# Feed-forward weights in seven-product units: sums by adding transfers in place of GpSimd subtractions

## The chip, the cores and the metric

The kernel runs on one core of a Trainium2 chip. The metric is the device time of one execution in microseconds. TensorE (PE) does the matrix products, ScalarE (ACT) and VectorE (DVE) work along rows, GpSimd (POOL) is a third elementwise engine, and SyncE (SP) issues most transfers.

## The reference

The kernel computes two decoder layers over a sequence of 512 tokens of width 1024 in fp32. Layer 0 mixes with a causal convolution, layer 1 with differential attention. Behind each follow a SwiGLU feed-forward block of inner width 2816 and a gated embedding. The change concerns the feed-forward block alone:

```python
def swiglu(x, w_gate, w_up, w_down):
    return (jax.nn.silu(x @ w_gate) * (x @ w_up)) @ w_down

h = h + swiglu(rms_norm(h, ffn_norm_g[i]), ffn_w_gate[i], ffn_w_up[i], ffn_w_down[i])
```

## The kernel before

All activations are held transposed, as eight chunks of 128 features by 512 tokens. Every fp32 operand is split into a high part, rounded to the matrix format by ScalarE (a cast), and a low part, the remainder, which VectorE subtracts. A product is then three matmuls (low by high, high by high, high by low; lines 166 to 168).

The inner width of 2816 is 22 chunks, taken in three parts of 6, 8 and 8 (`PARTS`). The first part is computed plainly. The second and third go in *units*. A unit computes two chunks of one matrix (a `Gate` unit or an `Up` unit) as a 2 x 2 block product: the weights are blocks A11, A12, A21, A22 of 512 by 128, the normalized activations are blocks B11, B12, B21, B22 of 512 by 256. Seven block products in place of eight give the four result blocks. They need four sums of weight blocks (S1 to S4) and four sums of activation blocks (T1 to T4). The T sums are made once per layer in `Operands.chunk`, the S sums once per unit. A part of 8 chunks is 8 units, Gate and Up in turn, so each layer has 16 units and the kernel 32.

For a unit, `load` (lines 699 to 706) fetches two raw tiles of 512 KB each through SyncE's queue: r0 holds A11 and A12, r1 holds A21 and A22. Gate units use the tiles A0 and A1, Up units two slots of `wraw`. `prep` then makes the operands in six steps:

- step 0 splits A11 and A12 (a 1024-wide cast, line 710, and a 1024-wide subtraction, line 711);
- step 1 makes S1 = A21 + A22 and S2 = S1 - A11 on GpSimd (lines 720 and 721);
- step 2 splits S1 and S2;
- step 3 makes S3 = A11 - A21 into a tile of its own (line 732) and S4 = A12 - S2 into A21's place (line 733), on GpSimd;
- step 4 splits S3 alone (512 wide, lines 736 and 737);
- step 5 splits S4 and A22 together.

The pairs of 1024 go to four buffers each (`whi`, `wlo`); S3's pair goes to the tiles A4 and A5 in turn. `p(i)` does product i, 12 pairs of weight load and matmul, and what follows from its result: copies out of PSUM by ScalarE (lines 760, 765, 767), additions by VectorE (lines 762, 768, 773), and `ready`, which applies Silu (line 783) or multiplies Gate by Up (line 794). Within a unit the products go in the order 1, 2, 6, 5, 7; products 4 and 3, which use A22 and S4, are put off into the next unit, behind its products 2 and 6. So a unit's stretch is 1, 2, 4 of the last, 6, 3 of the last, 5, 7. While one unit's products run, `run` traces the next unit's `prep` between them.

The order of instructions on each engine is made when the kernel is built, from the order of the code and estimated times of readiness; an engine then works its queue in order. The first unit of each part is prepared during the down projection of the part before it, at the places that `HOOKS` lists (output chunk: steps).

Of the kernel before, what the change touches and what calls it, by code (L numbers as in the profile page):

```python
# [14 lines left out]
AF = mybir.ActivationFunctionType  # L15
ALU = mybir.AluOpType
# [4 lines left out]
P = 128  # L21
S = 512
# [56 lines left out]
LA = 4  # L79
PACK = True  # L80
OPS_AT = (1, 2, 4, 5)
HOOKS = {5: (None,), 6: (1, 3), 7: (0, 2, 4, 5)}
HT = S // 2
E1 = True
GLO = 1
# [6 lines left out]
def trunk(ctx, tc, xT, pT, wts, diag, dww, vec, rel, onehot, lamv, out):  # L92
    nc = tc.nc
    V, A, G, T = nc.vector, nc.scalar, nc.gpsimd, nc.tensor
# [7 lines left out]
    def sb(shape, tag, bufs, dt=F32):  # L102
        uid[0] += 1
        return pool.tile(shape, dt, tag=tag, name=f"{tag}_{uid[0]}", bufs=bufs)
# [10 lines left out]
    f = lambda ap: ap.bitcast(F32)  # L115
# [6 lines left out]
    def col(name, i=0):  # L122
        a, _ = VEC[name]
        return vt[:, a + i : a + i + 1]
# [9 lines left out]
    t = wk()[:, 0:P]  # L134
# [4 lines left out]
    t = tp()  # L139
# [49 lines left out]
    def both(t):  # L189
        return t[:, 0], t[:, 1]  # L190
# [18 lines left out]
    class Norm:  # L209
# [11 lines left out]
        def chunk(self, c):  # L221
            self.split(c)
            if c == 0:
                self.acc = sb([P, S], "acc", 1)
                A.activation(self.acc, h[c], AF.Square)
            else:
                sq = wk()
                self.square = A.activation(sq, h[c], AF.Square)  # L228
                self.last = self.eng.tensor_tensor(self.acc, self.acc, sq, ALU.add)  # L229
# [57 lines left out]
    def load(c):  # L287
        return lambda: nc.sync.dma_start(h[c], xT[c])
# [308 lines left out]
    with tc.manual_schedule(engines={V.engine, A.engine}):  # L597
        for c in range(NC + 2):
            if c < NC:
# [3 lines left out]
                hi = A.copy(z[c][0], y[c])  # L603
            if c >= 2:
                lo = V.tensor_tensor(z[c - 2][1], y[c - 2], f(z[c - 2][0]), ALU.subtract)
# [46 lines left out]
    class Operands:  # L652
# [10 lines left out]
        def chunk(self, k, rb):  # L663
            ub = sb([P, 2, S], "B6", 1)
            u1, u2 = both(ub)
            for c, u in ((k, u1), (k + 4, u2)):
                V.scalar_tensor_tensor(u, h[c], col(self.norm.g, c), rb, ALU.mult, ALU.mult)
            (u11, u12), (u21, u22) = ((u[:, :HT], u[:, HT:]) for u in (u1, u2))
            hi1, lo1 = self.low[k]
            A.copy(hi1, u11)  # L670
            hi2, lo2 = self.uppers(k)
            A.copy(hi2, u2)
            t = sb([P, 4, HT], "B7", 1)
            V.tensor_tensor(t[:, 0], u12, u11, ALU.subtract)
            V.tensor_tensor(t[:, 1], u22, t[:, 0], ALU.subtract)
            V.tensor_tensor(t[:, 2], u22, u12, ALU.subtract)
            V.tensor_tensor(t[:, 3], u21, t[:, 1], ALU.subtract)
            hi, lo = self.tops(k)
            A.copy(hi, t)
            V.tensor_tensor(lo1, u11, f(hi1), ALU.subtract)  # L680
            self.at["B11"][k] = hi1, lo1
            V.tensor_tensor(lo2, u2, f(hi2), ALU.subtract)
            self.at["B21"][k] = hi2[:, :HT], lo2[:, :HT]
            self.at["B22"][k] = hi2[:, HT:], lo2[:, HT:]
            V.tensor_tensor(lo, t, f(hi), ALU.subtract)
            for i in range(4):
                self.at[f"T{i + 1}"][k] = hi[:, i], lo[:, i]

    class Unit:
# [9 lines left out]
        def load(self):  # L699
            self.raw = []  # L700
            for j in range(2):
                raw = sb([P, 2, S], *(("wraw", 2) if self.raws == "wraw" else (f"A{j}", 1)))
                nc.sync.dma_start(raw, wts[self.i + j].rearrange("p (j k) -> p j k", j=2))
                self.raw.append(raw)
            self.sums = sb([P, 2, S], f"A{2 + self.n % 2}", 1)
            self.s3 = sb([P, 2, S], f"A{6 + self.n % 2}", 1)[:, 0]

        def two(self, src, a, b):
            hi, lo = sb([P, 2, S], "whi", 4, F32R), sb([P, 2, S], "wlo", 4, F32R)
# [3 lines left out]
                self.w[n] = hi[:, j], lo[:, j]  # L713

        def prep(self, step):
            (r0, r1), s, s3 = self.raw, self.sums, self.s3
            if step == 0:
                self.two(r0, "A11", "A12")
            elif step == 1:
                G.tensor_tensor(s[:, 0], r1[:, 0], r1[:, 1], ALU.add)  # L720
                G.tensor_tensor(s[:, 1], s[:, 0], r0[:, 0], ALU.subtract)
            elif step == 2:
                if self.first:
                    for j in range(2):
                        hi, lo = wk(F32R), wk(F32R)
                        A.copy(hi, s[:, j])
                        V.tensor_tensor(lo, s[:, j], f(hi), ALU.subtract)
                        self.w[f"S{j + 1}"] = hi, lo
                else:
                    self.two(s, "S1", "S2")  # L730
            elif step == 3:
                G.tensor_tensor(s3, r0[:, 0], r1[:, 0], ALU.subtract)
                G.tensor_tensor(r1[:, 0], r0[:, 1], s[:, 1], ALU.subtract)
            elif step == 4:
                hi, lo = both(sb([P, 2, S], f"A{4 + self.n % 2}", 1, F32R))
                A.copy(hi, s3)
                V.tensor_tensor(lo, s3, f(hi), ALU.subtract)
                self.w["S3"] = hi, lo
            else:
                self.two(r1, "S4", "A22")  # L740

        def product(self, acc, w, b, first):
            for k in range(4):
# [4 lines left out]
        def p(self, i):  # L748
            if i == 1:
                self.a, self.c = mm(), mm()  # L750
            a, lo, hi = self.a[:, :HT], self.c[:, :HT], self.c[:, HT:]
            acc, w, b, first = {
                1: (a, "A11", "B11", True), 2: (hi, "A12", "B21", True), 6: (a, "S2", "T2", False),
                5: (lo, "S1", "T1", True), 7: (a, "S3", "T3", False), 4: (a, "A22", "T4", False),
                3: (lo, "S4", "B22", False),
            }[i]
            self.product(acc, w, b, first)
            o = self.out
            if i == 1:
                A.copy(o[0][:, :HT], a)  # L760
            elif i == 2:
                V.tensor_tensor(o[0][:, :HT], o[0][:, :HT], hi, ALU.add)
                self.ready(0, 0)
            elif i == 6:
                A.copy(o[0][:, HT:], a)
            elif i == 7:
                A.copy(o[1][:, HT:], a)
                V.tensor_tensor(o[1][:, HT:], o[1][:, HT:], lo, ALU.add)
                self.ready(1, 1)
            elif i == 4:  # L770
                self.ready(1, 0)
            elif i == 3:
                V.tensor_tensor(o[0][:, HT:], o[0][:, HT:], lo, ALU.add)
                self.ready(0, 1)

    class Gate(Unit):
# [3 lines left out]
        def ready(self, j, k):  # L780
            cut = slice(k * HT, (k + 1) * HT)
            src = self.a[:, :HT] if (j, k) == (1, 0) else self.out[j][:, cut]
            A.activation(self.out[j][:, cut], src, AF.Silu)

    class Up(Unit):
        def start(self):
# [3 lines left out]
        def ready(self, j, k):  # L790
            o, g = self.out[j], self.gate.out[j]
            cut = slice(k * HT, (k + 1) * HT)
            if j == 1:
                V.tensor_tensor(o[:, cut], self.a[:, :HT] if k == 0 else o[:, cut], g[:, cut], ALU.mult)
            self.done[j] += 1
            if self.done[j] < 2:
                return
            if j == 0:
                V.tensor_tensor(o, o, g, ALU.mult)
            hid = both(sb([P, 2, S], f"B{self.at + j}", 1, F32R))  # L800
            A.copy(hid[0], o)
            V.tensor_tensor(hid[1], o, f(hid[0]), ALU.subtract)
            self.hid[self.at + j] = hid

    def ffn(norm, after, spare):
# [14 lines left out]
        def run(us):  # L820
            for n, x in enumerate(us):
                last = us[n - 1] if n else None
                nxt = us[n + 1] if n + 1 < len(us) else None
                x.start()
                if nxt:
                    nxt.load()
                x.p(1)
                if nxt:
                    nxt.prep(0)
                x.p(2)  # L830
                if nxt:
                    nxt.prep(1)
                if last:
                    last.p(4)
                x.p(6)
                if nxt:
                    nxt.prep(2)
                if last:
                    last.p(3)
                x.p(5)  # L840
                if nxt:
                    nxt.prep(3)
                    nxt.prep(4)
                x.p(7)
                if nxt:
                    nxt.prep(5)
            us[-1].p(4)
            us[-1].p(3)

        us = None  # L850
        for at, (f0, n) in enumerate(PARTS):
# [34 lines left out]
            if at < len(PARTS) - 1:  # L886
# [6 lines left out]
                x = us[0]  # L893
                for m, steps in HOOKS.items():
                    hooks[m] = partial(lambda steps: [x.load() if k is None else x.prep(k) for k in steps], steps)
# [56 lines left out]
    for k in range(2):  # L952
        t = tp()
# [447 lines left out]
```

## Time and profile before

| | |
|---|---|
| median of 3 runs | 1249.71 us (1249.7 to 1250.26) |
| the profiled execution | 1249.66 us |
| its span | 1247.6 us |
| TensorE busy | 1236.4 us, 99% |
| VectorE busy | 877.6 us, 70% |
| ScalarE busy | 623.0 us, 50% |
| GpSimd busy | 470.5 us, 38% |
| granted TensorE clock | 0.999 |

The span is the part of the execution that the trace covers; the rest lies before and after it. A group of the profile is one line of the kernel, one engine, one operation and the tiles it writes and reads ("out<-in"), with the count, the busy time, the mean duration in ns, and the idle time of the engine just before.

### The profile page before, as it was taken

The numbers are of one execution on the slowest core, as the hardware profiler recorded it, in microseconds if no ns is written. First come the engines' busy times: TensorE is split into PE (matmuls) and PEld (weight loads), VectorE is DVE, ScalarE is ACT, GpSimd is POOL, SyncE is SP. The second block draws the span as 40 slices with busy tenths as digits, with TensorE's granted clock in tenths as the row PEclk, the third lists the DMA queues.
The fourth block names the chain that finished last, engine by engine and source line by source line (L and its number), as shares of the span: only waits on it lengthen the run. The fifth ranks groups of instructions, "written<-read, shape, count | busy, mean of one in ns | idle before, by whom it ended". The sixth has DMA issues, their size and how long they took to land.

```text
span 1247.6 us, 18420 instructions
## 1 busy us (share of the span) xinstructions
PE 1236.4 (99%) x7080; PEld 1081.5 (87%) x7080; DVE 877.6 (70%) x1230; ACT 623.0 (50%) x1096; POOL 470.5 (38%) x355
## 2 busy tenths in 40 slices
PE   9999999999999999999999999999999999999998
PEld 7888788888998899888888888788889998999887
DVE  6998866985895478546676876646966885588535
ACT  5653464533553255334666877735434552455432
POOL 3763442024670365132346635041026640562220
PEclk9999999999999999999999999999999999999999
DMA  7566214324233322334432331142333333233321
GB/s 267 175 205 206 82 51 121 96 97 127 85 102 118 102 87 76 109 104 143 122 119 75 113 92 36 51 147 88 92 118 97 102 117 108 82 102 88 104 97 67
DMA packets 49154, 136.33 MB, mean 109 GB/s; under 512 B 5635, under 2 KB 10243, under 8 KB 49068
## 3 DMA queue, kind: packets, MB, share of 16 engines
q1 hardware_dynamic: 46944, 131.74, 33.7%
q10 hardware_dynamic: 2124, 3.43, 1.0%
q8 instruction: 55, 0.90, 0.3%
q14 instruction: 31, 0.25, 0.1%
HBM read 128.84 MB, written 6.31 MB: 108 GB/s over the span
## 4 chain that ended last, share of the span: by engine, by line
PE 88%; DVE 5%; issue 2%; DMA 1%; ACT 1%; SPq 0%; POOL 0%; DVEq 0%; ACTq 0%
PE mm L166 27%; PE mm L167 27%; PE mm L168 27%; PE mm L1117 1%; DVE sc L449 1%; DVE wlo L161 1%; PE sc L1085 1%; PE sc L1084 1%; PE tp L1104 1%; PE sc L398 1%; PE mm L398 1%; PE tp L1038 1%; PE mm L354 1%; PE tp L199 1%; DVE wlo L711 0%
## 5 line engine op out<-in xcount | busy, mean ns | idle before, releaser
L159 ACT CAST whi<-wraw 128x1024 fp32r<-128x1024 f32 (+2 forms) x145 | 145.6, 1013 | 220.2 <-PE mm L168 97.2
L161 DVE TENSOR_TENSOR wlo<-wraw,whi 128x1024 fp32r<-128x1024 f32 (+2 forms) x141 | 179.3, 1277 | 73.7 <-ACT whi L159 73.5
L166 PE MATMUL mm<-A,wlo 128*128 128x512 f32 (+1 forms) x568 | 222.5, 392 | 0.3 <-ACT A L206 0.2
L167 PE MATMUL mm<-A,whi 128*128 128x512 f32 (+1 forms) x568 | 219.8, 388 | 0.0
L168 PE MATMUL mm<-A,whi 128*128 128x512 f32 (+1 forms) x568 | 217.6, 389 | 0.0
L166 PE MATMUL mm<-B,wlo 128*128 128x512 f32 x352 | 137.9, 392 | 0.0
L167 PE MATMUL mm<-B,whi 128*128 128x512 f32 x352 | 137.8, 391 | 0.0
L168 PE MATMUL mm<-B,whi 128*128 128x512 f32 x352 | 136.2, 391 | 0.0
L229 POOL TENSOR_TENSOR acc<-acc,wk 128x512 f32<-128x512 f32 x35 | 58.3, 1665 | 194.5 <-ACT wk L228 193.9
L166 PEld LDWEIGHTS mm<-A,wlo 128*128 128x128 f32 x568 | 106.9, 188 | 23.6 <-issue 1.4
L167 PE MATMUL mm<-C,whi 128*128 128x256 f32 x448 | 127.0, 283 | 0.0
L168 PE MATMUL mm<-C,whi 128*128 128x256 f32 x448 | 127.0, 283 | 0.0
L166 PE MATMUL mm<-C,wlo 128*128 128x256 f32 x448 | 127.0, 283 | 0.0
L167 PEld LDWEIGHTS mm<-A,whi 128*128 128x128 f32 x568 | 107.0, 188 | 22.0 <-issue 1.0
L168 PEld LDWEIGHTS mm<-A,whi 128*128 128x128 f32 x568 | 106.6, 188 | 21.9 <-issue 0.5
L711 DVE TENSOR_TENSOR wlo<-A,whi 128x1024 fp32r<-128x1024 f32 x60 | 104.6, 1752 | 21.0 <-ACT whi L710 21.0
L710 ACT CAST whi<-A 128x1024 fp32r<-128x1024 f32 x60 | 62.9, 1048 | 56.6 <-PE mm L168 45.3
L720 POOL TENSOR_TENSOR A<-wraw 128x512 f32<-128x512 f32 x16 | 25.4, 1589 | 170.3 <-DMA wraw<-in_wts 156.1
L720 POOL TENSOR_TENSOR A<-A 128x512 f32<-128x512 f32 x16 | 25.3, 1581 | 161.9 <-DMA A<-in_wts 159.2
L167 PEld LDWEIGHTS mm<-C,whi 128*128 128x128 f32 x448 | 86.1, 192 | 0.2
L166 PEld LDWEIGHTS mm<-C,wlo 128*128 128x128 f32 x448 | 86.1, 192 | 0.2
L168 PEld LDWEIGHTS mm<-C,whi 128*128 128x128 f32 x448 | 86.1, 192 | 0.0
(309 smaller groups left out, 3030.6 us busy)
## 6 DMA issues: line engine op xcount, KB each, us to landing
wraw<-in_wts SPq DMA_DIRECT2D x161, 512.0 KB, 3.6
A<-in_wts SPq DMA_DIRECT2D x32, 512.0 KB, 3.6
wraw<-in_wts SPq DMA_DIRECT2D x16, 384.0 KB, 3.1
D<-in_diag SPq DMA_DIRECT2D x22, 256.0 KB, 4.7
C<-in_diag SPq DMA_DIRECT2D x16, 256.0 KB, 4.4
h<-in_xT SPq DMA_DIRECT2D x8, 256.0 KB, 5.2
rest<-h SPq DMA_DIRECT2D x8, 256.0 KB, 2.5
bias<-scr ACTq DMA_DIRECT2D x8, 256.0 KB, 3.7
```

The lines of the kernel that those rows point to most:

```text
L159: A.copy(hi[:, cut], raw[:, cut])
L161: eng.tensor_tensor(lo[:, cut], raw[:, cut], f(hi[:, cut]), ALU.subtract)
L166: T.matmul(acc, al, bh, start=first, stop=False, **kw)
L167: T.matmul(acc, ah, bh, start=False, stop=False, **kw)
L168: return T.matmul(acc, ah, bl, start=False, stop=last, **kw)
L199: r = T.matmul(t[:, cut], src[:, cut], ones, start=first and b == 0, stop=last and b == 3)
L229: self.last = self.eng.tensor_tensor(self.acc, self.acc, sq, ALU.add)
L354: last_tap[0] = T.matmul(acc, dg[:, j % 4], ups[c][:, j : j + S], start=(j == 0), stop=(j == PE_TAPS[c] - 1))
L398: last_tap[0] = T.matmul(acc[:, g * P : (g + 1) * P], w, ups[c][:, g, LEAD - m : LEAD - m + P], start=(m == 0), stop=(m == LAGS - 1),)
L710: A.copy(hi, src)
L711: V.tensor_tensor(lo, src, f(hi), ALU.subtract)
L720: G.tensor_tensor(s[:, 0], r1[:, 0], r1[:, 1], ALU.add)
```

## The change

The signs of the blocks are chosen anew, so that every weight sum is an addition: S2 = S1 + A11, S3 = A21 + A11, S4 = A12 + S2. To fit, B11's split is taken of the negated block, T1 and T2 are formed with other signs, and where results are combined a subtraction or a factor of -1 puts the sign right. VectorE's plain subtractions become scalar-tensor-tensor instructions there.

S1 and S2 stay on GpSimd. S3 and S4 are made by transfers that add into their destination: A11 is added into A21's place in r1, and S2 into A12's place in r0. They are issued from GpSimd's queue. The tile for S3 (`s3`) goes. S3 and A22 now stand side by side in r1 and are split together (step 4); S4 is split alone into A4 or A5 (step 6). The order of steps is 0, 1, 2, 3, 5, 4 before product 7 and 6 behind it; in the first unit of a part 1, 3, then 0, 2, 5, 4, 6.

```diff
-HOOKS = {5: (None,), 6: (1, 3), 7: (0, 2, 4, 5)}
+HOOKS = {5: (None,), 6: (1, 3), 7: (0, 2, 5, 4, 6)}
...
-            A.copy(hi1, u11)
+            A.activation(hi1, u11, AF.Copy, scale=-1.0)
...
-            V.tensor_tensor(t[:, 0], u12, u11, ALU.subtract)
-            V.tensor_tensor(t[:, 1], u22, t[:, 0], ALU.subtract)
+            V.scalar_tensor_tensor(t[:, 0], u11, -1.0, u12, ALU.mult, ALU.subtract)
+            V.scalar_tensor_tensor(t[:, 1], t[:, 0], -1.0, u22, ALU.mult, ALU.subtract)
...
-            V.tensor_tensor(lo1, u11, f(hi1), ALU.subtract)
+            V.scalar_tensor_tensor(lo1, u11, -1.0, f(hi1), ALU.mult, ALU.subtract)
...
-            self.s3 = sb([P, 2, S], f"A{6 + self.n % 2}", 1)[:, 0]
...
-                G.tensor_tensor(s[:, 1], s[:, 0], r0[:, 0], ALU.subtract)
+                G.tensor_tensor(s[:, 1], s[:, 0], r0[:, 0], ALU.add)
...
             elif step == 3:
-                G.tensor_tensor(s3, r0[:, 0], r1[:, 0], ALU.subtract)
-                G.tensor_tensor(r1[:, 0], r0[:, 1], s[:, 1], ALU.subtract)
+                G.dma_start(r1[:, 0], r0[:, 0], accum_op=ALU.add)
             elif step == 4:
+                self.two(r1, "S3", "A22")
+            elif step == 5:
+                G.dma_start(r0[:, 1], s[:, 1], accum_op=ALU.add)
+            else:
                 hi, lo = both(sb([P, 2, S], f"A{4 + self.n % 2}", 1, F32R))
-                A.copy(hi, s3)
-                V.tensor_tensor(lo, s3, f(hi), ALU.subtract)
-                self.w["S3"] = hi, lo
-            else:
-                self.two(r1, "S4", "A22")
+                A.copy(hi, r0[:, 1])
+                V.tensor_tensor(lo, r0[:, 1], f(hi), ALU.subtract)
+                self.w["S4"] = hi, lo
...
-                V.tensor_tensor(o[0][:, :HT], o[0][:, :HT], hi, ALU.add)
+                V.tensor_tensor(o[0][:, :HT], hi, o[0][:, :HT], ALU.subtract)
...
-            A.activation(self.out[j][:, cut], src, AF.Silu)
+            A.activation(self.out[j][:, cut], src, AF.Silu, scale=-1.0 if (j, k) == (1, 1) else 1.0)
...
-                V.tensor_tensor(o[:, cut], self.a[:, :HT] if k == 0 else o[:, cut], g[:, cut], ALU.mult)
+            if j == 1 and k == 0:
+                V.tensor_tensor(o[:, cut], self.a[:, :HT], g[:, cut], ALU.mult)
+            elif j == 1:
+                V.scalar_tensor_tensor(o[:, cut], o[:, cut], -1.0, g[:, cut], ALU.mult, ALU.mult)
...
                 if nxt:
                     nxt.prep(3)
+                    nxt.prep(5)
                     nxt.prep(4)
                 x.p(7)
                 if nxt:
-                    nxt.prep(5)
+                    nxt.prep(6)
```

More of the change, by code (lines that the diff above doesn't have):

```diff
@@ L715, in prep @@
         def prep(self, step):
-            (r0, r1), s, s3 = self.raw, self.sums, self.s3
+            (r0, r1), s = self.raw, self.sums
             if step == 0:
@@ L792, in ready @@
             cut = slice(k * HT, (k + 1) * HT)
-            if j == 1:
-                V.tensor_tensor(o[:, cut], self.a[:, :HT] if k == 0 else o[:, cut], g[:, cut], ALU.mult)
+            if j == 1 and k == 0:
+                V.tensor_tensor(o[:, cut], self.a[:, :HT], g[:, cut], ALU.mult)
+            elif j == 1:
+                V.scalar_tensor_tensor(o[:, cut], o[:, cut], -1.0, g[:, cut], ALU.mult, ALU.mult)
             self.done[j] += 1
```

## The prediction

> **What bounds the kernel now.** I read the page first: the span, the engines' shares and the chain.
>
> ```profile
> span 1247.6 us, 18420 instructions
> ...
> PE 1236.4 (99%) x7080; PEld 1081.5 (87%) x7080; DVE 877.6 (70%) x1230; ACT 623.0 (50%) x1096; POOL 470.5 (38%) x355
> ...
> PE 88%; DVE 5%; issue 2%; DMA 1%; ACT 1%; SPq 0%; POOL 0%; DVEq 0%; ACTq 0%
> ```
>
> TensorE is busy in 99% of the span and is 88% of the chain that ended last; GpSimd, which loses work here, is busy 38% and 0% of the chain. The change touches only the four stretches in which the feed-forward weights go through in units of seven products, so I asked for the busy time in those four windows (columns: window, length, then each engine's busy time).
>
> ```profile
> 301.85:380.18 78.33, 77.97 (x650) 77.76 (x649) 64.43 (x67) 42.84 (x74) 48.90 (x28) 1.00 0.32 97
> 427.10:504.75 77.65, 77.65 (x650) 77.65 (x648) 60.16 (x66) 43.54 (x74) 37.57 (x22) 1.00 0.27 83
> 947.69:1025.74 78.05, 77.90 (x649) 77.70 (x648) 64.13 (x67) 42.89 (x74) 51.31 (x28) 1.00 0.32 97
> 1072.67:1150.38 77.71, 77.71 (x649) 77.69 (x648) 60.67 (x66) 42.77 (x74) 36.88 (x22) 1.00 0.28 83
> sum 311.74, PE 311.24 PEld 310.80 DVE 249.40 ACT 172.04 POOL 174.66; mean PE 77.81 PEld 77.70 DVE 62.35 ACT 43.01 POOL 43.67
> ```
>
> There TensorE is idle 311.74 - 311.24 = 0.5 us in all. The timeline shows the grid it runs on: the first matmul of two consecutive units (product 1 begins with the tile wth), and product 6 of the first of them.
>
> ```profile
> 454.42 0.28 PE L166 MATMUL mm<-wth,wlo 128*128 128x256 f32 x1
> ...
> 458.72 0.28 PE L166 MATMUL mm<-C,wlo 128*128 128x256 f32 x1
> ...
> 464.48 0.28 PE L166 MATMUL mm<-wth,wlo 128*128 128x256 f32 x1
> ```
>
> A unit takes 464.48 - 454.42 = 10.06 us for 7 x 4 x 3 = 84 matmuls, 0.120 us each. The windows hold 4 x 648 on that grid, 310.4 us, so all that waits can cost there is 311.74 - 310.4 = 1.3 us. That is the ceiling of any gain in the stage. The list of TensorE's waits over the whole run agrees, and has the larger ones elsewhere:
>
> ```profile
> PE sc L1084 <- DVE st L1087: 1.3, 2, 1.0
> ...
> PE tp L1147 <- ACT wtl L1106: 0.6, 1, 0.6
> ...
> PE mm L166 <- DVE big L768: 0.4, 1, 0.4
> ```
>
> Only the last is in a unit; the other two are in attention.
>
> **The change part by part.** *The two sums that leave GpSimd.* The groups kept apart by shape:
>
> ```profile
> L733 POOL TENSOR_TENSOR A<-A,A 128x512 f32<-128x512 f32 x16 | 30.2, 1885 | 1.3
> ...
> L733 POOL TENSOR_TENSOR wraw<-wraw,A 128x512 f32<-128x512 f32 x16 | 29.2, 1826 | 1.3
> ...
> L721 POOL TENSOR_TENSOR A<-A,wraw 128x512 f32<-128x512 f32 x16 | 29.0, 1813 | 0.0
> ...
> L732 POOL TENSOR_TENSOR A<-wraw,wraw 128x512 f32<-128x512 f32 x16 | 29.0, 1811 | 0.0
> ...
> L732 POOL TENSOR_TENSOR A<-A,A 128x512 f32<-128x512 f32 x16 | 26.9, 1679 | 0.0
> ...
> L267 POOL TENSOR_TENSOR r<-v,mhalf 128x4 f32<-128x4 f32 x7 | 8.1, 1150 | 35.2 <-DVE v L265 35.2
> ```
>
> L732 and L733 fall away: 30.2 + 29.2 + 29.0 + 26.9 = 115.3 us of GpSimd. No wait of TensorE in these windows names GpSimd, so this is worth 0. Each unit instead issues two adding transfers on GpSimd. The trace has no transfer issued by GpSimd and none that adds. Issue is bounded by SyncE's 0.33 us (row below) and by the longest sum it replaces, 1.89; I take 1.15, the small GpSimd instruction L267. Even 2 x 1.89 and the two remaining sums, 1.81 each by L721, are 7.4 us of a 10.06 us unit. Landing:
>
> ```profile
> 445.71 0.33 SPq L703 DMA_DIRECT2D A<-in_wts  x1
> ...
> A<-in_wts SPq DMA_DIRECT2D x32, 512.0 KB, 3.6
> ...
> rest<-h SPq DMA_DIRECT2D x8, 256.0 KB, 2.5
> ...
> out_t<-h SPq DMA_DIRECT2D x7, 256.0 KB, 2.0
> ...
> wk<-in_lamv ACTq DMA_DIRECT2D x1, 128.0 KB, 5.7
> ```
>
> From 2.0 (the quickest 256 KB) to 5.7 us (the slowest row). I take 2.5, the nearest in size and source. Issue and landing are then 2.3 to 7.6, taken as 3.65 us. The adds use the same 16 DMA engines: beside 1 MB loaded per unit they read at most 2 x 2 x 256 KB, another 1 MB, so the DMA share of 0.27 to 0.32 in the windows could double and still leave a third free; cost to the loads 0.
>
> *What waits for the adds.* S3 is added into A21's place as soon as S1 has read A21, and S4 into A12's place when S2 is there and A12 has been split by ScalarE and VectorE. So r0, the tile with A11 and A12, used to be free after that split and is now held until S4's own split is done; the next load but one for that slot starts later. Rows of one Gate tile, whose unit starts at 464.48 (the last but one is a longest split, of another unit; the last the next sum on GpSimd):
>
> ```profile
> 460.16 1.23 DVE L711 TENSOR_TENSOR wlo<-A,whi 128x1024 fp32r<-128x1024 f32 x1 [0.49 <-ACT whi L710]
> ...
> 461.45 5.30 SPq L703 DMA_DIRECT2D A<-in_wts  x2
> ...
> 461.86 1.05 ACT L710 CAST whi<-A 128x1024 fp32r<-128x1024 f32 x1 [1.12 <-PE mm L168]
> ...
> 465.35 0.62 ACT L736 CAST A<-A 128x512 fp32r<-128x512 f32 x1 [0.30 <-POOL A L732]
> ...
> 466.65 1.44 DVE L737 TENSOR_TENSOR A<-A,A 128x512 fp32r<-128x512 f32 x1
> ...
> 454.35 2.32 DVE L711 TENSOR_TENSOR wlo<-A,whi 128x1024 fp32r<-128x1024 f32 x1
> ...
> 461.74 1.29 POOL L720 TENSOR_TENSOR A<-wraw 128x512 f32<-128x512 f32 x1 [6.15 <-DMA wraw<-in_wts]
> ```
>
> Before, the split ends at 460.16 + 1.23 = 461.39 and the load goes at 461.45. Now: 461.39 + (2.3 to 7.6) for the add + 0.62 + 1.44 for the split = 465.8 to 471.1, and landed 3.6 later, 469.4 to 474.7. The unit that uses it starts two units on, at 464.48 + 2 x 10.06 = 484.6, and its split (1.05 + at most 2.32) must begin by 481.2. At the worst end 6.5 us are left, so I cost the later load at 0; if that cover were gone, every second unit would wait. S2's sum, done by 474.7 + 1.8 (L721) = 476.5, isn't needed in split form before product 6, 458.72 - 454.42 = 4.3 us into the unit. The whole round of r0 (load 3.6, split 3.4, add at most 7.6, split 2.1) is 16.7 us of the 20.1 it has.
>
> *GpSimd's queue.* The add of S4 waits on GpSimd for the split of A12, which ends at 461.39; behind it stand the sums of the following unit. Those begin at 461.74 and their unit starts at 464.48 + 10.06 = 474.5, so an issue of 0.33 to 1.89 ahead of them costs 0.
>
> *The casts and splits.* The 1024-wide pair is now S3 with A22 and the 512-wide one S4 alone: the same number of ScalarE casts and VectorE splits. S3 is due at product 7, A22 and S4 one unit later. The pair's buffer goes free after product 4 rather than 3, 2.9 us earlier, a small help to the split of A11 and A12 that reuses such buffers. Cost 0.
>
> *Signs.* Three VectorE instructions in each of eight operand chunks, and the last Up product, become scalar-tensor-tensor.
>
> ```profile
> L667 DVE SCALAR_TENSOR_TENSOR B<-h,vec,rb 128x512 f32<-128x512 f32 x8 | 5.6, 748 | 0.1
> ...
> L682 DVE TENSOR_TENSOR C<-B,C 128x512 fp32r<-128x512 f32 x3 | 2.1, 684 | 0.0
> ```
>
> That is at most 748 - 684 = 64 ns each, 40 x 0.064 = 2.6 us of VectorE over the run, under a TensorE that didn't wait for it. The scale of -1 in eight ScalarE copies and in sixteen Silus rides on instructions that are there anyway: 0. In the other direction VectorE's splits should get shorter, because they overlap fewer sums:
>
> ```profile
> L711 DVE TENSOR_TENSOR wlo<-A,whi x60: 1217/1708/2379, 290.9 to 1140.5; 128x1024 fp32r<-128x1024 f32 x60
> ```
>
> If all 60 came down from the median to the minimum, 60 x 0.49 = 29 us of VectorE; also off the path.
>
> *A rule against the change.* The splits and adds in the unit windows are TENSOR_TENSOR rows, as L711 and L737 above. The Trainium skill (SBUF — State Buffer, the passage on the trap by which VectorE blocks a DMA) says that a transfer issued by GpSimd has its descriptors written by GpSimd, which is locked out while VectorE runs a copy-like instruction in a two-port mode, and gives 620 ns becoming about 3100 ns. By that rule an add would be later by one VectorE instruction; by the trace's kind of instruction it doesn't apply.
>
> **The sum.** The profiled execution took 1249.66 us: the span of 1247.6 and 2.06 around it; the median of the runs is 1249.71. Units 0 (bounds -1.3 and the rival's price), GpSimd 0, signs 0, start and end of the program with one more queue 0 (bounds 0 and the present 2.06 again). Forecast 1249.7 us, for itself 1248.4 to 1251.8.
>
> **The rivals.** *ScalarE held by a landing (slower).* The order of each engine's instructions is fixed when the kernel is built. If the cast of S3 with A22, or of S4, stands at the head of ScalarE's queue and its add hasn't landed, the copies of the products out of PSUM stand behind it, and product 6 may not go on with the bank before product 1 is copied:
>
> ```profile
> 456.05 0.37 ACT L760 COPY wk<-mm 128x256 f32<-128x256 f32 x1 [0.17 <-PE mm L168]
> ```
>
> That copy ends at 456.42 and product 6 begins at 458.72: 2.3 us of cover. If the order was made for 3.65 us, TensorE loses time from 3.65 + 2.3 = 6.0 us on; at the bound of 7.6 it loses 1.6 us an add. At one add in eight, 8 x 1.6 = 13 us: 1262.5; at half of the 64, 51 us: 1301. For it: everything that the add costs is unmeasured here, and there are 64. Against: only three such copies fall in a unit, and no row above reaches 6 us to land. Chance 0.23.
>
> *Starved issue (slower).* If VectorE does hold up GpSimd's descriptors, by its longest L711 of 2.38 us, the add takes 3.65 + 2.38 = 6.03, just at the threshold; twice per unit at some 0.1 us is 6 us: 1256. This is the rule of the Trainium skill named above. Chance 0.04.
>
> *r0 held too long (slower).* If the add and the queues ahead of the casts take over 3.4 us more than the 16.7 us round, every second unit waits; 1 us in 16 units is 1266. Chance 0.04.
>
> *The added queue costs time at start or end (slower).* Over the present 2.06 again: 1252.5. Chance 0.03.
>
> *Order elsewhere (faster).* The same builder places attention after these stages; if its waits of 1.3 and 0.6 us went, and the 1.3 of the units, 3.2 us: 1246.5. Only by luck of order. Chance 0.06.
>
> *The adds hold GpSimd as long as the sums did*, so that it isn't relieved at all: still 7.4 us of 10.06, within the forecast.
>
> **How the numbers follow.** The forecast has 0.60. Some 0.2% (2.5 us) is what a measurement of this kernel can tell from no change. Faster 0.06; slower 0.23 + 0.04 + 0.04 + 0.03 = 0.34; the rest same. The range of 8 in 10 leaves out half of the faster case (0.03), the held queue beyond one add in eight (0.12) and the late r0 (0.04), 0.19 in all: 1247.5 to 1262.5.
>
> **What would show it.** Right: the four windows at 77.6 to 78.4 us with TensorE idle under 1.5 us in all; GpSimd down by 42 us (64 issues of 1.15) to 94 us (of 0.33); the adds landing in 2 to 6 us; L711 with a median nearer 1.2 than 1.7. Wrong: ScalarE waits on a landing, over 2.3 us long, ahead of a split, with TensorE waiting for L760, L765 or L767; or a unit's first product waiting for its split because the load came late; or a span that stays while the time around it grows.

## The result, and the profile after

The changed kernel takes 1271.75 us (median of 4 runs, 1268.2 to 1273.26) against 1249.7 us of the kernel before in the same session: a ratio of 1.0174, with a 95% interval of 1.0151 to 1.0197. That is 22 us slower, above the range of 1247.5 to 1262.5. The prediction was wrong; the first rival, ScalarE held by a landing, is what happened, at a price between the two that it gave. The profiled execution took 1272.38 us, 1.78 us of it outside the span.

The page of the changed kernel, the lines that answer to those of before:

```profile
span 1270.6 us, 18512 instructions
...
PE 1243.9 (98%) x7080; PEld 1086.0 (85%) x7080; DVE 835.5 (66%) x1230; ACT 619.8 (49%) x1096; POOL 395.0 (31%) x355
...
PE 76%; DMA 10%; DVE 6%; issue 2%; ACT 2%; POOL 1%; SPq 0%; POOLq 0%; ACTq 0%; DVEq 0%
```

In the chain that ended last, DMA has gone from 1% to 10% and TensorE from 88% to 76%. The span grew by 1270.6 - 1247.6 = 23.0 us. TensorE's time outside matmuls was 1247.6 - 1236.4 = 11.2 us and is now 1270.6 - 1243.9 = 26.7: 15.5 us of the growth. The other 7.5 us are the same 7080 matmuls, busy for longer (1243.9 against 1236.4); the last section returns to them.

The windows of the four unit stretches (same columns as before; a few matmuls of the down projection lie inside them too):

```profile
302.25:391.19 88.94, 83.00 (x657) 82.05 (x656) 58.35 (x70) 44.24 (x77) 30.75 (x28) 0.96 0.54 139
436.28:518.16 81.88, 78.67 (x650) 77.85 (x648) 51.94 (x67) 42.25 (x74) 24.16 (x23) 1.00 0.51 126
961.04:1048.56 87.52, 82.58 (x658) 81.00 (x657) 58.52 (x70) 43.38 (x76) 31.20 (x28) 0.98 0.55 141
1093.65:1173.37 79.72, 78.47 (x650) 77.86 (x648) 51.88 (x67) 42.11 (x74) 24.11 (x23) 1.00 0.51 128
sum 338.06, PE 322.72 PEld 318.77 DVE 220.69 ACT 171.97 POOL 110.23; mean PE 80.68 PEld 79.69 DVE 55.17 ACT 42.99 POOL 27.56
```

The idle time is all here: 338.06 - 322.72 = 15.3 us where it was 0.5. Every engine but TensorE has the same work as before or less, and no engine is near its limit. So this is a wait, not a load. The list of waits names it (engine, what it was about to do, whom it waited for: us in total, times, longest):

```profile
DVE A L739 <- ACT A L738: 64.9, 28, 5.9
...
ACT A L738 <- DMA wraw<-A: 43.7, 15, 5.9
ACT A L738 <- DMA A<-A: 38.4, 14, 6.5
...
PE mm L166 <- ACT big L760: 7.6, 4, 3.5
PE mm L166 <- ACT big L767: 4.9, 4, 1.9
PE mm L166 <- ACT wk L767: 1.2, 2, 0.7
...
PE mm L166 <- ACT wk L760: 0.7, 2, 0.4
```

Line 738 is the cast of S4 (the code's step 6). ScalarE sat in front of it for 43.7 + 38.4 = 82.1 us, in 29 of its 32 executions, until the transfer that adds S2 into A12's place had landed. Lines 760 and 767 are the copies of products 1 and 7 out of PSUM, and TensorE waited for these 12 times, 14.4 us in all. One such place, on ScalarE:

```profile
355.23 0.62 ACT L803 CAST B<-wk 128x512 fp32r<-128x512 f32 x1
359.50 0.62 ACT L738 CAST A<-wraw 128x512 fp32r<-128x512 f32 x1 [3.66 <-DMA wraw<-A]
360.03 0.36 ACT L767 COPY big<-mm 128x256 f32<-128x256 f32 x1
360.29 0.38 ACT L760 COPY wk<-mm 128x256 f32<-128x256 f32 x1
```

on GpSimd, which issued that transfer behind a sum of the next unit,

```profile
354.71 1.28 POOL L719 TENSOR_TENSOR A<-A 128x512 f32<-128x512 f32 x1 [6.24 <-DMA A<-in_wts]
355.95 0.86 POOL L735 DMA_DIRECT2D wraw<-A  x1
```

and on TensorE:

```profile
358.22 0.28 PE L168 MATMUL mm<-C,whi 128*128 128x256 f32 x1
360.44 0.39 PE L166 MATMUL mm<-C,wlo 128*128 128x256 f32 x1 [1.95 <-ACT big L767]
```

The cast is next on ScalarE from 355.84; the transfer is issued at 355.95 and has landed by 359.50, 3.55 us later. The copies of products 7 and 1 stand behind the cast. In the code product 4 goes on in the bank of product 7, and product 6 in that of product 1, so neither may begin before that copy; product 4 is due first, and TensorE stops for 1.95 us. The cast itself was in no hurry: the product that uses this S4 begins at 374.97 on TensorE.

The add was late as well. VectorE had ended the split of A12 at 350.39 + 1.22 = 351.61, but GpSimd stood until 354.71 at the sum shown, which waited 6.24 us for the next unit's load. In 8 of the 32 units the add stands directly behind a sum for which GpSimd had waited 5.8 us or more.

### The profile page after: what moved, and what is told of

Its sections match the earlier page's. It is cut to its first block, busy times and chain, and to the rows that moved or that the text cites. A ratio compares the mean times of both kernels' runs of the same rounds, so it can differ in the third digit from the quotient of the medians.

```text
span 1270.6 us, 18512 instructions
## 1 busy us (share of the span) xinstructions
PE 1243.9 (98%) x7080; PEld 1086.0 (85%) x7080; DVE 835.5 (66%) x1230; ACT 619.8 (49%) x1096; POOL 395.0 (31%) x355
## 4 chain that ended last, share of the span: by engine, by line
PE 76%; DMA 10%; DVE 6%; issue 2%; ACT 2%; POOL 1%; SPq 0%; POOLq 0%; ACTq 0%; DVEq 0%
PE mm L166 23%; PE mm L167 23%; PE mm L168 23%; DMA wraw<-A 3%; DMA A<-in_wts 3%; DMA A<-A 2%; DMA wraw<-in_wts 1%; PE mm L1120 1%; DVE sc L449 1%; DVE wlo L161 1%; DVE wlo L710 1%; PE sc L1088 1%; PE sc L1087 1%; PE tp L1107 1%; PE sc L398 1%
## 5 line engine op out<-in xcount | busy, mean ns | idle before, releaser
L166 PE MATMUL mm<-C,wlo 128*128 128x256 f32 x528 | 150.6, 286 | 6.9 <-ACT big L767 4.9
L167 PE MATMUL mm<-C,whi 128*128 128x256 f32 x528 | 149.7, 284 | 0.0
L168 PE MATMUL mm<-C,whi 128*128 128x256 f32 x528 | 149.6, 284 | 0.0
L166 PEld LDWEIGHTS mm<-C,wlo 128*128 128x128 f32 x528 | 101.5, 193 | 9.1 <-ACT big L767 6.1
L167 PEld LDWEIGHTS mm<-C,whi 128*128 128x128 f32 x528 | 101.8, 193 | 0.2
L168 PEld LDWEIGHTS mm<-C,whi 128*128 128x128 f32 x528 | 101.7, 193 | 0.0
L710 DVE TENSOR_TENSOR wlo<-A,whi 128x1024 fp32r<-128x1024 f32 x60 | 79.2, 1320 | 22.5 <-ACT whi L709 21.9
L719 POOL TENSOR_TENSOR A<-A 128x512 f32<-128x512 f32 x16 | 22.5, 1403 | 194.7 <-DMA A<-in_wts 174.7
L884 DVE TENSOR_TENSOR h<-mm,h 128x512 f32<-128x512 f32 x48 | 32.9, 689 | 73.0 <-PE mm L168 72.8
```

The costliest lines, as they stand in the source:

```text
L166: T.matmul(acc, al, bh, start=first, stop=False, **kw)
L167: T.matmul(acc, ah, bh, start=False, stop=False, **kw)
L168: return T.matmul(acc, ah, bl, start=False, stop=last, **kw)
L710: V.tensor_tensor(lo, src, f(hi), ALU.subtract)
L884: V.tensor_tensor(h[m], acc, h[m], ALU.add)
```

## The experiments

The first four runs set out from the *length* theory ("Theory 1" in the expectations), which is the prediction's own rival: the place of the cast is right for a short sum, and an add of issue plus landing overruns it. Three rivals were held against it: r0, kept until S4 is split, and the new order of splits cost the time (Rival 2); each adding transfer costs alike, by its traffic (Rival 3); the signs cost it. The *place* theory ("Theory 1b") was put up only after these four: the cast stands too early on ScalarE whatever makes the sum. Rival 2b is Rival 2, held against it. All diffs are against the changed kernel. The order on each engine is made anew for each kernel, so what stands behind the cast can differ from one kernel to the next.

**The signs alone.** The sums are additions, but GpSimd makes them, S3 in a tile of its own and S4 in A21's place, in the old order of steps.

```diff
...
-                G.dma_start(r1[:, 0], r0[:, 0], accum_op=ALU.add)
+                G.tensor_tensor(s3, r0[:, 0], r1[:, 0], ALU.add)
+                G.tensor_tensor(r1[:, 0], r0[:, 1], s[:, 1], ALU.add)
...
```

> Only the signs of the change: S3 and S4 are additions on GpSimd in their old places (S3 in its own tile, S4 in A21's place), with the old order of steps; no transfer adds. Theory 1 (ScalarE's queue is held by the cast of S4, whose add lands after it is wanted): nothing of this is left, 1248.5 to 1251. Rival (the scalar-tensor-tensor instructions and scales cost the time): 1255 to 1272.

Measured: 1249.93 us (10 runs), ratio 1.0000 (0.9991 to 1.0010). The signs cost nothing that shows, and nothing of the 22 us is theirs.

**Both in-place sums by GpSimd.** Places and order of the change, without a transfer.

```diff
-                G.dma_start(r1[:, 0], r0[:, 0], accum_op=ALU.add)
+                G.tensor_tensor(r1[:, 0], r1[:, 0], r0[:, 0], ALU.add)
...
-                G.dma_start(r0[:, 1], s[:, 1], accum_op=ALU.add)
+                G.tensor_tensor(r0[:, 1], r0[:, 1], s[:, 1], ALU.add)
```

> All of the change, with its order of steps and its places, but both in-place sums are made by GpSimd additions (about 1.3 to 1.8 us each) in place of adding transfers (3.3 to 4.3 us from issue to the cast of S4). Theory 1: the cast of S4 waits some 2 us less, TensorE's waits for L760 and L767 fall under 4 us in all, 1250 to 1256. Rival 2 (holding r0 until S4 is split and the new order of splits cost the time, whoever adds): 1266 to 1272.

Measured: 1268.64 us (4 runs), ratio 1.0156 (1.0141 to 1.0171). Its waits:

```profile
ACT A L738 <- POOL wraw L735: 55.2, 16, 5.5
...
ACT A L738 <- POOL A L735: 40.9, 12, 6.5
...
PE mm L166 <- ACT big L767: 11.3, 9, 2.7
```

Without any landing ScalarE waits 96 us at the same cast and TensorE behind the same copies. Without a transfer in it, the kernel keeps 19 of the 22 us. The length theory, which expected 1256 at most, falls here. The time lies in the range of Rival 2, so whether the place or the held r0 costs it was still open.

**One sum each.** S3 by transfer and S4 by GpSimd in place, and the reverse.

> The change with S4's in-place sum on GpSimd; only S3 is added by a transfer. Theory 1 (S4's add): 1250 to 1256, as with both on GpSimd. Rival 3 (each adding transfer costs alike, through DMA traffic that delays the weight loads): about half of the 22 us, 1259 to 1263.

> The change with S3's in-place sum on GpSimd; only S4 is added by a transfer. Theory 1 (S4's add): 1266 to 1274, ScalarE waits at S4's cast 60 to 90 us in all, as in the change. Rival 3: 1259 to 1263.

Measured: S4 by GpSimd 1265.63 us (4 runs), ratio 1.0125 (1.0107 to 1.0142); S3 by GpSimd 1281.87 us (4 runs), ratio 1.0254 (1.0236 to 1.0273). Each lies above both of the ranges given for it. Both wait at line 738, for 91 and 92 us. Of the pair of transfers S4's is the dearer at this place (1281.87 against 1268.64, with S3 on GpSimd in both), but the two effects do not add up: taking S3's transfer away from the change made it 10 us slower. ScalarE's wait is of one size in the four kernels (82, 96, 91 and 92 us) and TensorE's loss is not. It may be that other copies stand behind the waits; that was not followed up, and the differences between the four stay open.

**The cast behind a copy.** The cast of S4 moves into the unit's own stretch: it is asked for after product 6, and tied on ScalarE behind the copy of product 6.

```diff
-HOOKS = {5: (None,), 6: (1, 3), 7: (0, 2, 5, 4, 6)}
+HOOKS = {5: (None,), 6: (1, 3), 7: (0, 2, 5, 4)}
...
-                A.copy(hi, r0[:, 1])
+                with tc.issue_after(self.copied.ins):
+                    A.copy(hi, r0[:, 1])
...
-                A.copy(o[0][:, HT:], a)
+                self.copied = A.copy(o[0][:, HT:], a)
...
                 x.p(6)
+                x.prep(6)
...
                 x.p(7)
-                if nxt:
-                    nxt.prep(6)
```

> The change, transfers and all, with one thing moved: ScalarE's cast of a unit's S4 stands behind that unit's own copy of product 6 (line 765 of the change), some 5 us later in ScalarE's queue; S4 is due one unit later still. Theory 1b (not the length of the add but the place of S4's cast in ScalarE's queue, ahead of the copies out of PSUM, while the chain split of A12, add, landing ends after that): the cast waits under 20 us in all (82 us in the change), TensorE hardly waits for L760 and L767, 1249 to 1253. Rival 2b (r0 held until S4 is split makes the loads and the sums late): r0 is held longer still, so 1272 or slower.

Measured: 1248.44 us (10 runs), ratio 0.9989 (0.9979 to 0.9998). The page, and the cast on ScalarE, now at line 739:

```profile
span 1246.5 us, 18518 instructions
...
PE 1235.1 (99%) x7080; PEld 1080.3 (87%) x7080; DVE 824.3 (66%) x1230; ACT 623.0 (50%) x1096; POOL 396.5 (32%) x355
...
346.76 0.86 POOL L735 DMA_DIRECT2D wraw<-A  x1
...
355.34 0.37 ACT L766 COPY wk<-mm 128x256 f32<-128x256 f32 x1
355.61 0.63 ACT L739 CAST A<-wraw 128x512 fp32r<-128x512 f32 x1
```

The cast runs 355.61 - 346.76 = 8.85 us after the issue and finds the sum there. No wait at line 739 is left in the trace and no wait of TensorE in a unit. TensorE is idle for 1246.5 - 1235.1 = 11.4 us, as much as before the change. The time is just below the range of the place theory and far from that of Rival 2b, although r0 is held longer here. The transfers are those of the change, and S4's land about as late (median 3.5 us from the issue, 3.8 in the change); in the code only the place of one split differs, and it is worth 23 us. With the waits above, that shows the place theory.

**The wait moved to another engine.** The cast at its old place in the order, but on GpSimd:

```diff
-                A.copy(hi, r0[:, 1])
+                G.tensor_copy(hi, r0[:, 1])
```

> The change with the cast of S4 on GpSimd in place of ScalarE; all else as in the change, r0 is held as long or longer. Theory 1b: ScalarE no longer waits for S4, so TensorE's waits for its copies go, 1249 to 1255. Rival 2b: 1266 to 1275.

Measured: 1252.64 us (10 runs, 1249.2 to 1257.11), ratio 1.0024 (1.0009 to 1.0040). GpSimd now stands in front of line 738, for 26.7 us at wraw alone (38.6 with the waits at A):

```profile
POOL A L738 <- DMA wraw<-A: 26.7, 9, 5.9
...
PE mm L166 <- DVE wk L762: 1.7, 1, 1.7
```

No PSUM copy queues behind it there, and most of the loss is gone. So it is the copies behind the cast that carry most of the loss, not the late operand.

**S4 in a tile of its own.** S3 stays a transfer; GpSimd writes S4 into a tile that nothing else reads, so r0 is free as early as before the change.

```diff
+            self.s4 = sb([P, 2, S], f"A{6 + self.n % 2}", 1)[:, 0]
...
-                G.dma_start(r0[:, 1], s[:, 1], accum_op=ALU.add)
+                G.tensor_tensor(self.s4, r0[:, 1], s[:, 1], ALU.add)
...
-                A.copy(hi, r0[:, 1])
-                V.tensor_tensor(lo, r0[:, 1], f(hi), ALU.subtract)
+                A.copy(hi, self.s4)
+                V.tensor_tensor(lo, self.s4, f(hi), ALU.subtract)
```

> S3 by an adding transfer as in the change, but S4 = A12 + S2 is made by GpSimd in a tile of its own, so that it waits neither for the split of A12 nor holds r0 until its own split. The order of splits is the change's. Theory 1b: the sum is ready long before ScalarE's cast, 1249 to 1252. If the joint split of S3 and A22, or S3's transfer, costs by itself: above 1255.

Measured: 1251.53 us (10 runs), ratio 1.0013 (1.0003 to 1.0023). ScalarE waits for that sum 6 times where it waited for the add 29 times (the execution profiled is the slowest of the ten, 1254.81 us):

```profile
ACT A L739 <- POOL A L736: 18.8, 6, 5.9
...
PE mm L166 <- ACT big L768: 2.0, 6, 0.3
```

A sum into its own tile need not wait until the split has read A12, and a sum in place has to. That points to the place on ScalarE being too early for a sum in place, whoever makes it.

**GpSimd sums at the good place.** The cast behind the copy of product 6, both sums in place by GpSimd.

> As the variant with S4's cast moved behind the unit's own copy of product 6, but both in-place sums on GpSimd (1268.6 without the move). Theory 1b: 1249 to 1253. Rival 2b: 1266 or slower.

Measured: 1262.06 us (4 runs), ratio 1.0097 (1.0082 to 1.0112), against 1248.44 with the transfers, between the ranges of both theories. Here the transfers do earn something: GpSimd is busy for 463.5 us against 396.5, and the casts wait for its sums.

```profile
POOL A L720 <- DMA A<-in_wts: 72.7, 14, 12.8
...
ACT whi L709 <- POOL A L720: 22.2, 12, 2.7
...
PE mm L166 <- ACT big L768: 8.9, 11, 1.2
```

The first line is a second limit: S2's sum waits for r0's load. r0 is free only once S4 is split. But the late load alone is not what costs, for with transfers at the same place the sum waits even longer, and ScalarE hardly at all for it:

```profile
POOL A L720 <- DMA A<-in_wts: 93.8, 14, 12.8
...
ACT whi L709 <- POOL A L720: 3.9, 7, 0.9
```

It is the late load together with GpSimd's longer work.

**Holding r0 for less and for longer.** The same move of the cast, tied behind the copy of product 1 (three products, 4.3 us, sooner), with GpSimd sums and with transfers; behind the copy of product 7 (4.3 us later), with transfers; and the version behind product 6 once more, for its size.

> The same place, behind the copy of product 1, with both in-place sums on GpSimd. Behind the copy of product 6 this took 1262.1, and ScalarE waited for S2's sum, which waited for the load into r0. Theory (holding r0 costs there): r0 free 4.3 us sooner gives that back, 1249 to 1254. Rival (GpSimd's sums are too long for the stage, wherever S4 is split): 1259 to 1263.

> The change with S4's cast behind the unit's own copy of product 1 (4.3 us earlier than behind that of product 6, so that r0 is free 4.3 us sooner). Where it stood behind the copy of product 6 it came 8 to 17 us after the add's issue; here 4 to 13 us, and the add lands after 3.3 to 4.3. Theory 1b: waits at the cast under 20 us in all, 1247.5 to 1251. If the edge helped only by chance of order, anything up to 1270.

> The change with S4's cast behind the unit's own copy of product 7, 4.3 us later than behind that of product 6: r0 is held 4.3 us more. Theory 2c (r0's round of load, split, add, split has little room left): the loads and S2's sums come late, ScalarE waits for S2's sum, 1255 to 1275. If r0 has the room that the prediction gave it (6.5 us at its worst end): 1247.5 to 1251.

> The variant with S4's cast behind the copy of product 6 once more, beside the three others: 1247.5 to 1249.5, and faster than the kernel before by 0.05 to 0.2%.

| sums, and the copy that S4's cast follows | us, median (runs) | ratio (95%) |
|---|---|---|
| GpSimd, product 1 | 1252.82 (11) | 1.0026 (1.0017 to 1.0035) |
| GpSimd, product 6 | 1262.06 (4) | 1.0097 (1.0082 to 1.0112) |
| transfers, product 1 | 1248.43 (11) | 0.9986 (0.9977 to 0.9995) |
| transfers, product 6, again | 1248.65 (11) | 0.9987 (0.9978 to 0.9996) |
| transfers, product 7 | 1282.61 (5) | 1.0254 (1.0233 to 1.0275) |

With GpSimd's sums the earlier place gives back 9 us, as the theory of the held r0 had it. The two places with transfers came out as expected. Behind product 7 the time is above even the slower of its two ranges: the cast never waits, and yet the kernel is the slowest of all. Its waits:

```profile
POOL A L720 <- DMA A<-in_wts: 147.3, 14, 16.8
...
ACT whi L709 <- DMA A<-in_wts: 29.7, 12, 4.4
...
PE mm L166 <- DVE wlo L710: 18.3, 12, 2.9
...
PE mm L166 <- ACT big L768: 6.6, 10, 1.2
```

Line 710 is the split that TensorE's first product needs. One round of r0 in that kernel, on ScalarE, SyncE's queue and TensorE:

```profile
336.12 0.62 ACT L739 CAST A<-A 128x512 fp32r<-128x512 f32 x1
...
343.98 1.04 ACT L709 CAST whi<-A 128x1024 fp32r<-128x1024 f32 x1 [4.16 <-DMA A<-in_wts]
...
338.17 0.33 SPq L703 DMA_DIRECT2D A<-in_wts  x1
...
346.34 0.58 PE L166 MATMUL mm<-wth,wlo 128*128 128x256 f32 x1 [2.61 <-DVE wlo L710]
```

S4's cast ends at 336.74, VectorE's half of the split follows, the load goes at 338.17, the split that waits for it begins 5.8 us later at 343.98, and TensorE is 2.6 us late. The cast must thus follow the landing and still release r0 in time. Behind products 1 and 6 both hold, with transfers; behind product 7 the second fails, and ahead of the copies, as in the change, the first.

The versions behind products 1 and 6 beat both kernels: 0.9986 and, in two sessions, 0.9989 and 0.9987, all three intervals below 1. The gain is some 1.5 us. In the profiled executions 1.1 us of it lies between the first matmul of a layer's first part of units and that of its second (125.25 to 124.57 us in layer 0, 124.98 to 124.56 in layer 1), where the prediction's ceiling of 1.3 us lay; another 0.3 us lies outside the span (2.06 to 1.8).

## Why the prediction was wrong, point by point

**The step that failed.** The forecast's own line for casts and splits, "the same number of ScalarE casts and VectorE splits ... Cost 0", counted instructions and not their place; and the rival began from "If the order was made for 3.65 us, TensorE loses time from 3.65 + 2.3 = 6.0 us on". It was taken for granted that the order leaves room for the chain split of A12, GpSimd's queue, issue, landing, and that only an overrun beyond it costs. In fact the cast stood ahead of the end of the chain in 29 of 32 units, 82.1 / 29 = 2.8 us in the mean, and by 96 us in all with no transfer in the chain. Of the sum 3.65 + 2.3 it was the first term that failed: ScalarE was free for the cast 1.4 us after the add's issue in the median of the 32 (from 2.1 us ahead of it to 4.5 behind), and no add landed in under 3.2. The cover of 2.3 us was about right: eleven of TensorE's twelve stops follow a cast that had waited 1.99 to 5.92 us (the twelfth follows one whose wait the profile puts down to a matmul), and shorter waits reached no matmul. But the prediction showed the cover of product 1's copy alone, and 6.1 of the 14.4 us were lost behind product 7's. The term for GpSimd's queue had a wrong order too: it put the add ahead of the next unit's sums, and in the place shown it came behind one that waited for a load. The prediction gave each cause a price per add; the diff itself had the sign to look for: step 6 is asked for directly behind product 7, whose copy is one of the two that were held.

**The terms of the sum.** The add was sized well: issue 0.87 (taken 1.15), landing from issue 3.2 to 6.2 us with a median of 3.8 for S4 (bounds of issue and landing together 2.3 to 7.6). The lines of the two transfers, S3's and then S4's, in the changed kernel, and the landing of the second from its issue:

```profile
L731 POOL DMA_DIRECT2D A<-A x16: 857/873/1202, 273.2 to 1143.6; - x16
...
L735 POOL DMA_DIRECT2D A<-A x16: 859/868/1200, 295.6 to 1149.0; - x16
...
DMA to landing us min/median/max: 3.2/3.8/6.2
```

Issue plus landing as the prediction added them is the landing here, which is counted from the issue's start: 3.8 against 3.65. The terms for GpSimd (470.5 down to 395.0, 75.5 us, foretold 42 to 94), the signs (0, by the run with signs alone) and the start and end (2.06 us then, 1.78 now) hold.

**VectorE's splits.** They came down as foretold, off the path as said; what that is worth alone no run shows:

```profile
L710 DVE TENSOR_TENSOR wlo<-A,whi x60: 1208/1226/2348, 291.3 to 1158.9; 128x1024 fp32r<-128x1024 f32 x60
```

The median is 1226 ns where it was 1708.

**The rivals.** ScalarE held by a landing: right in mechanism, place and sign, given 0.23 where the rest of the evidence (all of the add's cost unmeasured, three copies a unit, a fixed order) deserved more; the range left out its dearer part, and there the time fell. Its prices of 1262.5 and 1301 lie on both sides of 1271.75, but by another count: not one add in eight over a threshold, but nearly all S4 casts waiting and a dozen waits reaching TensorE by the list. Starved issue: the issue took 0.87 us in the median and 1.2 at most, so nothing of the 2.38 us by which VectorE was to hold it. Its price of 1256 was also too high by its own numbers: 6.03 - 6.0 is 0.03 us an add, some 2 us for 64, not 6. The condition of the Trainium skill's rule (SBUF — State Buffer, the trap) was not met by these TENSOR_TENSOR instructions, as the prediction said. r0 held too long: not the cause in the changed kernel, where TensorE waited 0.9 us for line 710 in all, but a real limit, and the 6.5 us that the prediction had left at the worst end were about right. In the round shown for the place behind product 7, the add is issued at 322.65 and the cast comes 13.5 us later, where the worst end had 7.6, and the load takes 5.8 us, not 3.6: 5.9 + 2.2 = 8.1 us, 1.6 too many. The loads did get longer in the changed kernel (from 3.6 to 4.1 us in the median of the 32 into A, with the DMA share at 0.51 to 0.55 where it was 0.27 to 0.32), but "cost to the loads 0" held for the time within those 0.9 us.

**What would show it.** The sign named for "wrong" is what the trace has: ScalarE waiting on a landing ahead of a split, with TensorE waiting for lines 760 and 767. The mark "over 2.3 us long" was near the truth: waits at the cast are as short as 1.2 us, but the shortest behind which TensorE stopped was 1.99.

## What to carry to other kernels

When a step is made slower or given another operand, look first at where its consumer stands in the queue of an in-order engine, and what stands behind it; here a wait for one operand that TensorE needed only some 15 us later held the copies that TensorE needed at once. A small cast is best put behind the copies that others wait for, and its latest place is where it still releases its source in time for the next load; between the two bounds the time was flat (1248.43 and 1248.65), outside them it cost 23 and 34 us. An adding transfer is then worth having: behind the copies of products 1 and 6 it was 4 and 14 us faster than the sum in place on GpSimd. At the place of the change it was 3 us slower, and against the kernel before the whole gain is some 1.5 us.

## What the hardware showed that was not expected

A stall of TensorE can cost twice. After the longest one in the changed kernel the matmuls do not go on at 0.12 us each:

```profile
311.19 0.58 PE L166 MATMUL mm<-C,wk 128*128 128x256 f32 x1 [3.50 <-ACT big L760]
311.57 0.41 PE L167 MATMUL mm<-C,wk 128*128 128x256 f32 x1
311.78 0.41 PE L168 MATMUL mm<-C,wk 128*128 128x256 f32 x1
311.99 0.41 PE L166 MATMUL mm<-C,wk 128*128 128x256 f32 x1
```

They step by 0.21 us until 314.13; in the window from 311 to 314 the granted clock is 0.50. From 311.19 on, 13 steps take 2.94 us where 13 x 0.12 would be 1.56, some 1.4 us extra. The stall of 2.96 us that ended at 969.32 was followed by such a stretch as well (17 long steps, 1.6 us), and so was that of 1.95 us at 360.44, though there the long steps begin only at 361.86 (17 with the first one, 1.6 us); one of 1.66 us was followed by a single long step. The three stretches are in the windows whose clocks are 0.96 and 0.98, and with 4.6 us they are most of the 7.5 us by which TensorE was busier. The Trainium skill (TensorE: Matmul & The Clock Gate, the part on the clock gate) has the half clock, after at least one idle window of about 3.4 us; the half step agrees, but here it followed stalls of 1.95 and 2.96 us as well, shorter than that. Why some stalls bring it and others not was not tried.

The adding transfer itself, 256 KB within SBUF, was cheap to issue: 0.87 us of GpSimd in place of 1.7 to 1.9 us of a sum, and it landed 3.2 us after its issue at the soonest.
